# A hybrid decoder layer on one core: where the MLP operands of the first 1024 tokens are made, and how the last tiles are ordered and stored

## The chip, the cores and the metric

The kernel runs on one core of a Trainium2 chip. The metric is the device time of one execution in microseconds. Before the change the median of three runs is 1920.23 us (1919.95 to 1920.85). Lower is better.

The engines that matter: TensorE (PE in the profile, with its weight loads as PEld), VectorE (DVE), ScalarE (ACT), GpSimd (POOL), and the queues of SyncE (SP), ScalarE and GpSimd that issue transfers between HBM and the on-chip memory SBUF. PSUM is the memory that TensorE writes, here eight banks of 128 x 512 fp32.

## The reference

One decoder layer over 2048 tokens of width 1024, all in fp32:

```python
h = rms_norm(x, attn_norm_g)
z = h @ w_in                        # q, k, v and three convolution parts
q, k = rms_norm(q, q_norm_g), rms_norm(k, k_norm_g)
y_attn = swa_sink_attention(q, k, v, sinks)        # causal window of 128
y_conv = gate_b * short_conv(gate_c * xc, conv_w)  # three taps
y = concat([rms_norm(y_attn, attn_out_g), rms_norm(y_conv, conv_out_g)])
x = x + y @ w_out
hm = rms_norm(x, mlp_norm_g)
x = x + square(relu(hm @ w_up)) @ w_down
```

The norm ahead of the MLP needs, for each token, the root mean square over its 1024 values, and for each channel the gain `mlp_norm_g`. `w_up` is 1024 x 4096, `w_down` 4096 x 1024.

## The kernel before, in words

**Products in three parts.** An operand is kept as a high part, rounded to the format fp32r, and a low part, the rest. A product is three matmuls: high x high, high x low, low x high (`mm3`, L272). A matmul of 128 x 512 is the unit.

**Mixers.** The tokens go through norm, input projection, attention, convolution and output projection in four chunks of 512 (`NCHUNK`), each four tiles of 128 rows (`NT`). For each chunk `mixers` (L1022) walks the four attention blocks; between their steps it calls `fill`, which takes so many steps from the generator `besides` (L978): what is left of the chunk before (its attention half of the output projection, `rest`), then this chunk's convolution products (`conv_pair`), then the convolution half of the output projection interleaved with the preparation of the next chunk, then the next chunk's q, k, v products. How many steps each `fill` takes stands in the table `FILL`. Weights are reloaded for each chunk by `weights` (L239) on SP's queue.

**Order.** The kernel is written in one program order; a scheduler, working ahead of time on a model, sets each engine's order by priority. `ahead(i)` (L195) shifts the priority of the instructions in it by the entry `i` of `PRIO` for the current chunk; a positive number is earlier, a negative one later, counted in instructions. Each engine and each queue then works strictly in its order. A tile of SBUF or PSUM with a tag has as many places as `bufs` says; a new tile of the tag waits until a place is free. The row tiles `xt` (128 x 1024) have two places; the PSUM tag `tr` has one bank.

**Output projection** (`out_projection`, L899). For each half `dh` of the 512 output columns and each tile `t`, four steps of three matmuls fill a bank `pout`; VectorE then adds it, scaled by the row's norm, into the residual row `x1[t]` (L925). The convolution half (`half` 1) comes first, the attention half (`half` 0) after it. With the last column half of the attention half the row is complete: it is stored to `x1_dram` (L932), and for the first three chunks its row norm is computed into `rs_x1` (L935). The weights `w_wo` of the last tile of chunk 3 go into the two places of the tag `raw`.

**The MLP by seven products.** Both MLP products use the seven products of Strassen's method over halves of 512 tokens and 512 channels. For tokens 0 to 1023 (`tb` 0), let b11 and b21 be the two channel halves of the normed, transposed first 512 tokens and b12 and b22 those of the second 512. The seven operands are b11, b21, b22 and four differences. They are stored in HBM, in `xop_dram`, by `x_put` (L335) on SP, a block of 128 x 512 at a time, and loaded and split by `load_x` (L409) when a product needs them.

**Where these operands are made before** (`prepare_mlp`, L940). In chunk 3, beside the convolution half of the output projection. For each of the eight row tiles of chunks 0 and 1 it reloads the row from `x1_dram` (L952), scales it on VectorE by row norm and gain (L290), transposes it in two groups of four 128 x 128 blocks on TensorE (L316), copies each bank to SBUF on ScalarE (L317), and stores blocks (L341) or, for a tile of chunk 1, first makes the four differences on VectorE (`x_sums`, L355). The blocks stand in the places that the chunk's operand `h` has left. `rs_x1` and the row of gains `g_mlp` are read.

**Start of the MLP** (`begin_mlp`, L434): the first x operand and four blocks of `w_up` (`wu_first`, in the scratch tag `s2`) are loaded as the last steps of `besides`. Tokens 1024 to 2047 are prepared during the up products (`prepare_rest`, L1236), with the gain as a column `g_cols`.

**The end** (L1537 on). The down products go through 7 x 8 steps; each step has for each `tb` four banks of six matmuls (L1552). With the last step of the last product, `last` (L1496) adds each bank to the sum in SBUF on VectorE (L1498) and stores 128 x 512 on SP (L1494).

Of the kernel before, what the change touches and what calls it, by code (L numbers as in the profile page):

```python
# [16 lines left out]
P = 128  # L17
# [17 lines left out]
CH = 512  # L35
# [47 lines left out]


PRIO = (
# [5 lines left out]
)  # L91

FILL = (
# [9 lines left out]
def hymba_layer(  # L103
# [225 lines left out]
    def turned(xb, k, dst, g, rs_row):  # L329
# [2 lines left out]
        d3, r3 = dst.rearrange("p (t q) -> p t q", t=NT), rs_row.rearrange("p (q t) -> p t q", t=NT)  # L332
        nc.vector.scalar_tensor_tensor(d3, d3, g, r3, op0=ALU.mult, op1=ALU.mult)

    def x_put(tb, t, i, b):  # L335

        dst = xop_dram[tb][ORDER.index(i)]
        if tb:
            nc.sync.dma_start(dst[:, t * BW : (t + 1) * BW], b)
        else:  # L340
            nc.sync.dma_start(  # L341
                dst.rearrange("p (h t c) -> p h t c", h=2, t=NB)[:, :, t], b.rearrange("p (h c) -> p h c", h=2)
            )

    def rs_out(c):

# [1 line left out]
            rs_dram[c].rearrange("(p t) -> p t", p=P), rs_x1[:, c * NT : (c + 1) * NT]  # L348
        )

    def x_sums(tb, t, b11, b21, b12, b22, t1):


        def sub(i, dst, a, b):
            nc.vector.tensor_tensor(dst, a, b, op=ALU.subtract)  # L355
            x_put(tb, t, i, dst)

        x_put(tb, t, 3, b22)
        sub(5, t1, b12, b11)
        sub(6, b11, b22, t1)  # L360
        sub(7, b12, b22, b12)
        sub(4, b21, b21, b11)

    def gain_row(g, name):
        gb = row("gb", name, 1)
# [243 lines left out]
    with tc.tile_pool(name="mix_small", bufs=1) as mix_small, tc.tile_pool(name="mix", bufs=1) as mix:  # L609
# [289 lines left out]
        def out_projection(c, half, ys, rs, x1):  # L899

            for dh in range(2):
                cs = slice(dh * 512, (dh + 1) * 512)
                hl = ahead_parts.pop((half, dh), None) or out_weights(c, half, dh)
                if half and dh and c + 1 == NCHUNK:
                    ahead_parts[0, 0] = out_weights(c, 0, 0)
                w4 = [w.rearrange("p (i c) -> p i c", i=NCT) for w in hl]
                order = [(t, i) for t in range(NT) for i in range(NCT)]
                if half and not dh:

                    order = sorted(order, key=lambda x: (x[0] == NT - 1, x[1] == NCT - 1))  # L910
                pss = {}
                for t, i in order:
                    if not i:
                        pss[t] = bank("mm", f"pout{c}_{half}_{dh}_{t}")
                    ps = pss[t]

                    def y(s, i=i, t=t):
                        return ys[i][:, s, t * P : (t + 1) * P] if half else ys[t][:, s, i, :]

                    mm3(ps, y, lambda s, i=i: w4[s][:, i, :], i == 0, i == NCT - 1)  # L920
                    if i < NCT - 1:
                        yield
                        continue
                    with ahead(11):
                        nc.vector.scalar_tensor_tensor(  # L925
                            x1[t][:, cs], ps, rs[:, t : t + 1], x1[t][:, cs], op0=ALU.mult, op1=ALU.add
                        )
                        if dh and not half:
                            r = (c * NT + t) * P

                            eng = nc.gpsimd if c + 1 == NCHUNK else nc.sync
                            eng.dma_start(x1_dram[r : r + P, :], x1[t])  # L932

                            if c + 1 < NCHUNK:
                                norm_stats(x1[t], f"m{c}_{t}", rs_x1[:, c * NT + t : c * NT + t + 1])  # L935
                                if t + 1 == NT and c == NCHUNK - 2:
                                    rs_out(c)
                    yield

        def prepare_mlp(gb):  # L940


            xs = [pool.tile([P, 8, CH], F32, tag=f"h{i}", name=f"xm{i}", bufs=1) for i in range(2)]
            xts = {}

            halves = lambda w: w.rearrange("p (k c) -> p k c", k=2)

            def fetch(n):
                t, i = tiles[n]
                r = i * CH + t * P  # L950
                xt = xs[1][:, 3::4] if n % 3 == 2 else halves(row("xt", f"xt_m{i}_{t}", 2))
                nc.sync.dma_start(xt, halves(x1_dram[r : r + P, :]))  # L952
                with ahead(8):
                    scaled(xt, rs_x1[:, r // P : r // P + 1], halves(gb))
                xts[t, i] = xt

            tiles = [(t, i) for i in range(2) for t in range(NT)]
            for n in range(3):
                fetch(n)
            yield  # L960
            for n, (t, i) in enumerate(tiles):
                b = [xs[0][:, 2 * t + k] for k in range(2)]
                if i:
                    b += [xs[1][:, 4 * (t % 2) + k] for k in range(3)]
                with ahead(9):
                    for _ in raised(xts[t, i], lambda k: b[2 * i + k], f"m{i}_{t}"):
                        pass

                if n + 3 < len(tiles):
                    fetch(n + 3)  # L970
                if i:
                    x_sums(0, t, *b)
                else:
                    x_put(0, t, 1, b[0])
                    x_put(0, t, 2, b[1])
                yield

        def besides(c, before, h, yt, rc, x1, h_next, z_next):  # L978

            yield from before  # L980
            ssc = mix.tile([P, CH], F32, tag="ssc", name=f"ssc{c}", bufs=1)
            for j in range(2):
                yield from conv_pair(c, h, j, yt, ssc)
            for t in range(NT):
                r = (c * NT + t) * P
                xr = row("x1", f"x1_{c}_{t}", NT)
                nc.sync.dma_start(xr, xf[r : r + P, :])
                x1.append(xr)
            out = out_projection(c, 1, yt, rc, x1)
            if c + 1 < NCHUNK:  # L990
                h_next += parts(pool, "h", f"h{c + 1}")
                steps = prepare(xf, (c + 1) * CH, g_row[0], h_next, f"a{c + 1}")
            else:
                steps = prepare_mlp(gain_row(mlp_norm_g, "g_mlp"))
            for i, _ in enumerate(steps):
                yield
                for j in range(STEPS):
                    next(out, None)
                    yield
                    if (i, j) == PC:  # L1000
                        pc = bank("tr", f"pc{c}")
                        for t in range(NT):
                            nc.tensor.matmul(
                                pc[:, t : t + 1], ssc[:, t * P : (t + 1) * P], mean, start=True, stop=True
                            )
                        ms = mix_small.tile([P, NT], F32, tag="msc", name=f"ms_c{c}", bufs=1)

                        with tc.high_priority(offset=SOON):
                            if c:
                                nc.vector.tensor_copy(ms, pc[:, :NT])  # L1010
                                rsqrt(rc, ms)
                            else:
                                nc.vector.tensor_tensor(ms, pc[:, :NT], rs0_2, op=ALU.mult)
                                rsqrt(rc, ms)
                                nc.gpsimd.tensor_tensor(rc, rc, rs0, op=ALU.mult)
            yield from out
            if c + 1 < NCHUNK:
                yield from project_qkv(c + 1, h_next, z_next)
            else:
                begin_mlp()  # L1020
# [458 lines left out]
    def down_out(tb, p, ps, v):  # L1479
# [14 lines left out]
            eng.dma_start(of[r0 : r0 + P, (k - 1) * BW : k * BW], b[:, j])  # L1494

        def last(i, k, b):  # L1496
            for j in range(NB):
                nc.vector.tensor_tensor(b[:, j], ps[j], b[:, j], op=ALU.add)  # L1498
                put(i, k, b, j)

        def plus(a, b):

# [37 lines left out]
    for i, (p, g) in enumerate(steps):  # L1540
# [5 lines left out]
        for tb in range(NTB):  # L1546
            if first and p not in GOES_ON:
                ps[tb] = banks(tb, f"d{p}_{tb}")
            for j in range(NB):
                for k in range(2):  # L1550
                    for n, (a, b) in enumerate(((0, 0), (0, 1), (1, 0))):
                        nc.tensor.matmul(  # L1552
                            ps[tb][j],
                            fs[tb][:, a, k, j * P : (j + 1) * P],
                            w[:, b, k, :],
                            start=first and p not in GOES_ON and k + n == 0,
                            stop=last and k + n == 3,
                            skip_group_check=True,
                        )
            if i == NCG // 4:  # L1560
                down_out(tb, p, None, vs[tb])
            if last:
# [29 lines left out]
```

## Time and profile before

| | |
|---|---|
| median of three runs | 1920.23 us |
| lowest, highest | 1919.95, 1920.85 us |
| the profiled execution | 1921.78 us |
| its span, first to last instruction | 1920.1 us |
| mixers, up to the last pout product | to about 702.8 us |
| up products | 702.8 to 1306.6 us |
| down products | 1306.6 to 1916.1 us |
| HBM read, written | 286.87 MB, 125.83 MB |

How to read the rows that follow. A group has line, engine, operation, output <- inputs by the program's names, tile shape and count; then busy us and mean ns of one; then idle time of the engine just before, and what ended it. A row of waits has who waited for whom: us in total, how often, the longest. A row of a timeline has start, duration, engine, line, operation; SPq is SP's queue. A row of windows has for each engine busy us, the count in brackets, then the granted TensorE clock (1.00 is full), the share in which the 16 DMA engines were busy, and GB/s. A line number can be that of a helper that several places call.

### The profile page before, as it was taken

How to read it: one execution, taken by the hardware profiler on the slowest of the kernel's cores; microseconds unless marked ns; L12 is line 12 of the kernel's file. 1: busy time of each engine (PE TensorE's matmuls, PEld its weight loads, DVE VectorE, ACT ScalarE, POOL GpSimd, SP SyncE). 2: the span in 40 equal slices, each digit the busy share in tenths (PEclk: the TensorE clock that was granted, in tenths of full speed). 3: DMA queues.
4: the chain of work that ended last, by engine and by line, in shares of the span. 5: the costliest groups of instructions: out<-in, count | busy, mean ns of one | idle time of the engine just before them, and what ended most of it. 6: DMA issues, size and time to landing. Idle time of an engine off the chain costs nothing.

```text
span 1920.1 us, 24578 instructions
## 1 busy us (share of the span) xinstructions
PE 1910.4 (99%) x8927; PEld 1588.8 (83%) x8927; DVE 1205.4 (63%) x1849; ACT 829.3 (43%) x1564; POOL 275.6 (14%) x477
## 2 busy tenths in 40 slices
PE   9999999999999999999999999999999999999999
PEld 8888888888888778888888888888888888888887
DVE  4895656548556769999887766766534334457541
ACT  6565434335344446454555545554332332232320
POOL 2122212302221112233100111111000000100000
PEclk9999999999999999999999999999999999999999
DMA  8984944564563897778665444438954456766631
GB/s 305 340 313 115 333 185 175 209 230 161 201 263 135 285 345 255 219 226 254 214 223 202 163 161 146 150 138 318 367 203 146 139 169 226 284 224 214 210 132 55
DMA packets 233048, 414.32 MB, mean 216 GB/s; under 512 B 51672, under 2 KB 136160, under 8 KB 220128
## 3 DMA queue, kind: packets, MB, share of 16 engines
q1 hardware_dynamic: 204096, 336.98, 51.7%
q0 software_dynamic: 15424, 51.40, 6.9%
q10 hardware_dynamic: 13408, 24.39, 3.4%
q8 instruction: 70, 1.15, 0.2%
q14 instruction: 50, 0.41, 0.1%
HBM read 286.87 MB, written 125.83 MB: 215 GB/s over the span
## 4 chain that ended last, share of the span: by engine, by line
PE 65%; DMA 1%; DVE 0%; POOL 0%; ACT 0%; issue 0%; SPq 0%; POOLq 0%; ACTq 0%
PE d L1552 32%; PE u L1445 32%; PE pout L276 0%; PE pout L274 0%; PE pout L275 0%; DMA w_wo<-wo 0%; DMA xop<-xm 0%; PE pt_m L316 0%; DVE xm L355 0%; POOL pp_b L745 0%; PE po_b L784 0%; DVE xm L290 0%; DVE xt_m L290 0%; ACT xm L317 0%; DVE x L925 0%; DVE o_b L793 0%
## 5 line engine op out<-in xcount | busy, mean ns | idle before, releaser
L1445 PE MATMUL u<-op_x,wop 128*128 128x512 f32 x2688 | 610.2, 389 | 0.0
L1552 PE MATMUL d<-op_w,op_f 128*128 128x512 f32 x2688 | 609.6, 389 | 0.0
L1445 PEld LDWEIGHTS u<-op_x,wop 128*128 128x128 f32 x2688 | 504.4, 188 | 105.4 <-issue 0.7
L1552 PEld LDWEIGHTS d<-op_w,op_f 128*128 128x128 f32 x2688 | 504.4, 188 | 105.0 <-DVE op_f L406 0.3
L406 DVE TENSOR_TENSOR op_f<-op_f 128x1024 fp32r<-128x1024 f32 x112 | 136.9, 1224 | 235.7 <-ACT op_f L405 235.5
L405 ACT CAST op_f<-op_f 128x1024 fp32r<-128x1024 f32 x112 | 117.6, 1051 | 354.0 <-DMA op_f<-fop 353.1
L425 DVE TENSOR_TENSOR wop<-wu,wop 128x512 fp32r<-128x512 f32 x156 | 110.7, 711 | 36.3 <-ACT wop L424 18.5
L424 ACT CAST wop<-wu 128x512 fp32r<-128x512 f32 x156 | 95.9, 619 | 85.5 <-PE u L1445 81.5
L1181 POOL DMA_DIRECT2D fop<-s x96 | 51.9, 541 | 440.3 <-DVE s L1184 435.8
L1187 DVE TENSOR_TENSOR u<-u,u 128x512 f32<-128x512 f32 x128 | 87.8, 686 | 21.6 <-PE u L1445 21.5
L406 DVE TENSOR_TENSOR op_w<-raw,op_w 128x1024 fp32r<-128x1024 f32 x56 | 68.4, 1222 | 25.7 <-ACT op_w L405 25.4
L405 ACT CAST op_w<-raw 128x1024 fp32r<-128x1024 f32 x56 | 58.8, 1052 | 44.6 <-PE d L1552 21.6
L1193 ACT ACTIVATE u<-u 128x512 f32<-128x512 f32 x64 | 40.5, 633 | 64.5 <-DVE u L1187 62.5
L713 ACT ACTIVATE sc_b<-sc_b,ngm_b 128x128 f32<-128x128 f32 x128 | 49.6, 389 | 27.0 <-DVE ngm_b L710 27.0
L745 POOL TENSOR_SCALAR_AFFINE_SELECT pp_b<-pp_b 128x512 fp32r<-128x512 f32 x60 | 42.3, 717 | 130.7 <-ACT pp_b L738 72.1
L1394 POOL DMA_DIRECT2D wds<-raw x16 | 8.6, 534 | 328.3 <-DVE raw L1392 328.3
L424 ACT CAST wop<-wu_s 128x512 fp32r<-128x512 f32 x64 | 39.7, 621 | 32.0 <-PE u L1445 24.9
L274 PE MATMUL pout<-w_wo,yt_c 128*128 128x512 f32 x128 | 52.4, 410 | 0.0
L274 PE MATMUL pout<-w_wo,at_b 128*128 128x512 f32 x128 | 50.3, 395 | 1.7 <-DMA w_wo<-wo 1.5
L276 PE MATMUL pout<-w_wo,yt_c 128*128 128x512 f32 x128 | 51.8, 405 | 0.0
L425 DVE TENSOR_TENSOR wop<-wu_s,wop 128x512 fp32r<-128x512 f32 x64 | 44.9, 704 | 9.9 <-ACT wop L424 9.7
L275 PE MATMUL pout<-w_wo,yt_c 128*128 128x512 f32 x128 | 50.9, 398 | 0.0
(264 smaller groups left out, 3106.0 us busy)
## 6 DMA issues: line engine op xcount, KB each, us to landing
op_f<-fop SPq DMA_DIRECT2D x112, 512.0 KB, 4.3
raw<-in_w_down_dram SPq DMA_DIRECT2D x72, 512.0 KB, 4.2
wu<-in_w_up_dram SPq DMA_DIRECT2D x128, 256.0 KB, 4.2
w_wo<-wo SPq DMA_DIRECT2D x24, 1024.0 KB, 6.8
fop<-s POOLq DMA_DIRECT2D x96, 256.0 KB, 2.7
fop<-u ACTq DMA_DIRECT2D x64, 256.0 KB, 2.6
op_x<-xop SPq DMA_DIRECT2D x28, 512.0 KB, 7.0
w_q<-q SPq DMA_DIRECT2D x12, 1024.0 KB, 6.6
```

The lines of the kernel that those rows point to most:

```text
L274: nc.tensor.matmul(ps, st(0), mv(0), start=first, stop=False)
L275: nc.tensor.matmul(ps, st(0), mv(1), start=False, stop=False)
L276: nc.tensor.matmul(ps, st(1), mv(0), start=False, stop=last)
L405: nc.scalar.copy(op[:, 0], raw)
L406: nc.vector.tensor_tensor(op[:, 1], raw, op[:, 0].bitcast(F32), op=ALU.subtract)
L424: splits.append(nc.scalar.copy(hi, blk).ins)
L425: nc.vector.tensor_tensor(lo, blk, hi.bitcast(F32), op=ALU.subtract)
L713: nc.scalar.activation(sc[:, hd, :], sc[:, hd, :], AF.Exp, bias=ngm[:, hd : hd + 1], accum_out=den[:, hd : hd + 1])
L1181: eng.dma_start(fop_dram[tb][ORDER_DOWN.index(i)][n // 2][:, n % 2], b)
L1187: return nc.vector.tensor_tensor(dst, ps, b, op=ALU.add).ins
L1445: nc.tensor.matmul(pt, wops[i][:, a, k, :], xops[tb, p][k // 2][:, b, k % 2, :], start=p not in GOES_ON and k + j == 0, stop=k + j == NB + ...
L1552: nc.tensor.matmul(ps[tb][j], fs[tb][:, a, k, j * P : (j + 1) * P], w[:, b, k, :], start=first and p not in GOES_ON and k + n == 0, stop=l ...
```

## The change

- The operands of `tb` 0 are made by `x_first` as soon as a row of chunk 0 or 1 is complete and its norm is known, from the row in SBUF. As the program order goes, that is in the part of the output projection that runs under the next chunk, so in chunks 1 and 2.
- ScalarE scales the row by its norm into a row tile `xt`; TensorE transposes it in two groups; VectorE multiplies each bank by the gain column `g_cols` straight back into the row tile.
- A tile of chunk 0 stores its two blocks (b11, b21). A tile of chunk 1 takes a second row tile, reloads these two from `xop_dram`, stores b22, and makes the four differences in place, storing each.
- `ahead(12)` and `ahead(13)` put this work 150 instructions later in priority in every chunk. `FILL` stays.
- `prepare_mlp` and its row of gains go; in chunk 3 three empty steps are left beside the convolution half.
- In chunk 3 ScalarE instead of VectorE copies the sums of squares `ms` (L1010).
- The last projection tile of chunk 3 (first row tile of the second column half) takes its eight products with the high weight part first, then the four with the low part.
- In the very last bank of the down products, the last three matmuls of 512 columns become six of 256, by column halves; the last addition and store are made in two halves, the second stored on ScalarE's queue.

```diff
@@ PRIO: two more entries, -150 and -150, in each of the five rows
-    (40, 0, 160, -10, 30, 0, 10, -10, -20, 30, 0, 300),
+    (40, 0, 160, -10, 30, 0, 10, -10, -20, 30, 0, 300, -150, -150),
...
+    def x_piece(tb, t, i):
+        return xop_dram[tb][ORDER.index(i)].rearrange("p (h t c) -> p h t c", h=2, t=NB)[:, :, t]
...
-    def x_sums(tb, t, b11, b21, b12, b22, t1):
...
+    def x_first(c, t, x1):
+        xt = row("xt", f"xt_m{c}_{t}", 2)
+        r = c * NT + t
+        with ahead(12):
+            nc.scalar.activation(xt, x1, AF.Copy, scale=rs_x1[:, r : r + 1])
+            for k in range(2):
+                pt = bank("tr", f"pt_m{c}_{t}_{k}").rearrange("p (j q) -> p j q", j=NB)
+                b = xt[:, k * BW : (k + 1) * BW]
+                for j in range(NB):
+                    nc.tensor.transpose(pt[:, j], b[:, j * P : (j + 1) * P], ident)
+                nc.vector.tensor_tensor(
+                    b.rearrange("p (j q) -> p j q", j=NB),
+                    pt,
+                    g_cols[:, k * NB : (k + 1) * NB, None].to_broadcast([P, NB, P]),
+                    op=ALU.mult,
+                )
+        x11, x12 = (xt[:, k * BW : (k + 1) * BW] for k in range(2))
+        if not c:
+            x_put(0, t, 1, x11)
+            x_put(0, t, 2, x12)
+            return
+        before = row("xt", f"xb_{t}", 2)
+        b11, b21 = (before[:, k * BW : (k + 1) * BW] for k in range(2))
+        for i, b in ((1, b11), (2, b21)):
+            nc.sync.dma_start(b.rearrange("p (h c) -> p h c", h=2), x_piece(0, t, i))
+        b12, b22 = x11, x12
+        x_put(0, t, 3, b22)
+        with ahead(13):
+            for i, dst, a, b in ((5, b11, b12, b11), (7, b12, b22, b12), (6, b22, b22, b11), (4, b21, b21, b22)):
+                nc.vector.tensor_tensor(dst, a, b, op=ALU.subtract)
+                x_put(0, t, i, dst)
...
@@ out_projection
+                hi_first = dh and not half and c + 1 == NCHUNK
...
-                    mm3(ps, y, lambda s, i=i: w4[s][:, i, :], i == 0, i == NCT - 1)
+                    if hi_first and t == 0:
+                        sums = [(a, 0, k) for k in range(NCT) for a in range(2)] + [(0, 1, k) for k in range(NCT)]
+                        for n in range(3 * i, 3 * i + 3):
+                            a, s, k = sums[n]
+                            nc.tensor.matmul(
+                                ps, ys[t][:, a, k, :], w4[s][:, k, :], start=n == 0, stop=n + 1 == len(sums)
+                            )
+                    else:
+                        mm3(ps, y, lambda s, i=i: w4[s][:, i, :], i == 0, i == NCT - 1)
...
                                 norm_stats(x1[t], f"m{c}_{t}", rs_x1[:, c * NT + t : c * NT + t + 1])
+                                if c < 2:
+                                    x_first(c, t, x1[t])
...
-        def prepare_mlp(gb):
...
@@ besides
-                steps = prepare_mlp(gain_row(mlp_norm_g, "g_mlp"))
+                steps = range(PC[0] + 1)
...
-                                nc.vector.tensor_copy(ms, pc[:, :NT])
+                                if c + 1 == NCHUNK:
+                                    nc.scalar.copy(ms, pc[:, :NT])
+                                else:
+                                    nc.vector.tensor_copy(ms, pc[:, :NT])
...
@@ last
-            for j in range(NB):
+            ends = tb + 1 == NTB and p == ORDER_DOWN[-1]
+            for j in range(NB - ends):
                 nc.vector.tensor_tensor(b[:, j], ps[j], b[:, j], op=ALU.add)
                 put(i, k, b, j)
+            if ends:
+                r0 = (2 * tb + i - 1) * BW + j * P + P
+                for eng, c in ((nc.sync, slice(0, BW // 2)), (nc.scalar, slice(BW // 2, BW))):
+                    x = b[:, NB - 1, c]
+                    nc.vector.tensor_tensor(x, ps[NB - 1][:, c], x, op=ALU.add)
+                    eng.dma_start(of[r0 : r0 + P, (k - 1) * BW + c.start : (k - 1) * BW + c.stop], x)
...
@@ the down products
+                sums = [(k, n, slice(0, BW)) for k in range(2) for n in range(3)]
+                if i + 1 == len(steps) and tb + 1 == NTB and j + 1 == NB:
+                    sums[3:] = [(1, n, slice(h * BW // 2, (h + 1) * BW // 2)) for h in range(2) for n in range(3)]
+                for k, n, cs in sums:
+                    a, b = ((0, 0), (0, 1), (1, 0))[n]
...
```

More of the change, by code (lines that the diff above doesn't have):

```diff
@@ L340, in x_put @@
         else:
-            nc.sync.dma_start(
-                dst.rearrange("p (h t c) -> p h t c", h=2, t=NB)[:, :, t], b.rearrange("p (h c) -> p h c", h=2)
-            )
+            nc.sync.dma_start(x_piece(tb, t, i), b.rearrange("p (h c) -> p h c", h=2))
     def rs_out(c):
@@ L349, in rs_out @@
         )
-    def x_sums(tb, t, b11, b21, b12, b22, t1):
[L354 to L362, printed above, removed]
+    def x_first(c, t, x1):
[29 more added lines that the diff above has]
+                x_put(0, t, i, dst)
     def gain_row(g, name):
@@ L938, in out_projection @@
                     yield
-        def prepare_mlp(gb):
[L943 to L976, printed above, removed]
         def besides(c, before, h, yt, rc, x1, h_next, z_next):
@@ L1549, in hymba_layer @@
             for j in range(NB):
[L1550 to L1559, printed above, removed]
+                sums = [(k, n, slice(0, BW)) for k in range(2) for n in range(3)]
[3 more added lines that the diff above has]
+                    a, b = ((0, 0), (0, 1), (1, 0))[n]
+                    nc.tensor.matmul(
+                        ps[tb][j][:, cs],
+                        fs[tb][:, a, k, j * P : (j + 1) * P],
+                        w[:, b, k, cs],
+                        start=first and p not in GOES_ON and k + n == 0,
+                        stop=last and k + n == 3,
+                        skip_group_check=True,
+                    )
             if i == NCG // 4:
```

8 rows, old and new, of the table PRIO are left out of this document.

## The prediction

> **What bounds the kernel now.** I read the page's busy shares and matmul groups first, then the windows around the last mixer chunk, then who waited for whom on TensorE, then the chain that ended last.
>
> ```profile
> span 1920.1 us, 24578 instructions
> PE 1910.4 (99%) x8927; PEld 1588.8 (83%) x8927; DVE 1205.4 (63%) x1849; ACT 829.3 (43%) x1564; POOL 275.6 (14%) x477
> L1445 PE MATMUL u<-op_x,wop 128*128 128x512 f32 x2688 | 610.2, 389 | 0.0
> ```
>
> TensorE is busy almost always. Nothing in the change takes a matmul away, so only its idle time can be won. That idle time lies in one place:
>
> ```profile
> 640.00:660.00 20.00, 19.39 (x111) 15.28 (x110) 14.33 (x22) 9.84 (x20) 3.80 (x6) 1.00 0.98 322
> 660.00:680.00 20.00, 19.16 (x96) 15.33 (x94) 19.29 (x33) 7.95 (x12) 5.26 (x6) 1.00 0.91 290
> 680.00:700.00 20.00, 18.53 (x82) 15.02 (x82) 9.06 (x13) 8.49 (x12) 1.97 (x4) 1.00 1.02 343
> 450.00:550.00 100.00, 99.81 (x530) 84.44 (x529) 63.25 (x118) 42.40 (x104) 30.45 (x46) 1.00 0.51 199
> ```
>
> After the times, the first column is TensorE, the third VectorE; the last two are the DMA share and GB/s. The end of chunk 3 idles 0.61 + 0.84 + 1.47 = 2.9 us in 60, the 100 us of chunk 2's end only 0.2. In the first, VectorE is at 96% for 20 us and the DMA engines are full.
>
> ```profile
> PE pout L274 <- DMA w_wo<-wo: 1.5, 1, 1.5
> PE po_b L784 <- POOL pp_b L745: 0.5, 1, 0.5
> PE pt_m L316 <- DVE ms_c L1010: 0.4, 1, 0.4
> PE pt_m L316 <- ACT xm L317: 0.3, 1, 0.3
> PE pa_b L805 <- DVE o_b L800: 0.3, 1, 0.3
> PE pt_m L316 <- DVE xt_m L290: 0.2, 1, 0.2
> ```
>
> These six are 3.2 us. A matmul is shown for 0.389 us but in a full stream one starts every 597.94 / 2638 = 0.227 us (next fence), so each wait hides up to 0.16 us more: about 4.2 us in all.
>
> ```profile
> 680.55 8.54 DMA w_wo<-wo
> 689.13 0.96 PE pout L274 x3
> 702.80 597.94 PE u L1445 x2638
> ...
> 647.10 0.44 PE pt_m L316 x4
> ...
> 675.48 2.32 SPq L341 DMA_DIRECT2D xop<-xm  x3
> 677.89 2.60 SPq L419 DMA_DIRECT2D wu_first<-in_w_up_dram  x4
> 680.55 3.45 SPq L245 DMA_DIRECT2D w_wo<-wo  x2
> ```
>
> The first four are the chain (the fourth shows four transposes in 0.44 us), the others SP's queue. The last projection weights are issued at 680.55 because SP holds the xop stores before them, and those wait for VectorE. From 702.8 on TensorE streams without a gap.
>
> **The change, part by part.** Times are changes to the runs' median, 1920.23 us; the profiled execution had a span of 1920.1 us and took 1921.78 us, so 1.7 us lie around its span. No step alters those.
>
> *Last projection weights.* The operand step leaves chunk 3, so its 28 stores leave SP's queue ahead of w_wo, and 7.3 MB of stores and 4.2 MB of reloads leave the full DMA engines. The reordered tile also starts on the high half alone. What is late next is the four wu_first loads, still ahead of w_wo and waiting for scratch rows. The wait of 1.47 + 0.16 goes: **-1.6** (ends: 0 if those loads hold SP as long; -1.63).
>
> *Waits of the old transposes.* 0.4 + 0.3 + 0.2 + 3 x 0.16 = **-1.4** (ends 0 and -1.4). Copying ms on ScalarE takes one more VectorE step away.
>
> *Other waits there.* po_b and pa_b: 0.5 + 0.3 + 2 x 0.16 = 1.1.
>
> ```profile
> L355 DVE TENSOR_TENSOR xm<-xm 128x512 f32<-128x512 f32 x12 | 7.8, 688 | 0.0
> L290 DVE SCALAR_TENSOR_TENSOR xt_m<-xt_m,rs_x,g_mlp 128x1024 f32<-128x1024 f32 x6 | 7.6, 1280 | 2.6 <-DMA xt_m<-x_dram 2.5
> L283 ACT ACTIVATE junk_m<-x 128x1024 bf16<-128x1024 f32 x12 | 12.7, 1056 | 47.3 <-DVE x L925 43.5 <-POOL rs_x L191 3.2 <-DVE ngm_b L710 0.6
> L317 ACT COPY xm<-pt_m 128x512 f32<-128x512 f32 x16 | 9.4, 587 | 12.0 <-PE pt_m L316 8.6 <-DMA xop<-xm 3.3
> L307 DVE TENSOR_TENSOR h_h<-pt_a,h_h 128x512 fp32r<-128x512 f32 x24 | 16.5, 687 | 3.3 <-ACT h_h L306 3.0
> L302 PE MATMUL pt_a<-ident,xt_a 128*128 128x128 f32 x96 | 14.5, 274 | 0.5 <-DVE h_h L307 0.2 <-DVE ms_b L807 0.2
> ```
>
> VectorE loses 16 subtractions of 0.69 and 8 scalings of 1.28, 21 us, ScalarE 16 copies of 0.59, so the attention chain behind them runs earlier. But 64 transposes, 7 us of cover at 0.11 each, go as well. I take half: **-0.55** (ends: +1.1, the waits doubled without cover; -1.1).
>
> *The same work in chunks 1 and 2.* Eight tiles, each with a ScalarE scaling of 128x1024 (1.06 by L283, for two copies of 0.59), eight transposes, two VectorE products from PSUM of 0.69 (the form of L307), and for four of them four subtractions: 11 + 11 us of VectorE beside 63% (450 to 550). TensorE does as many transposes as before. Their waits: the nearest row is L302, whose 24 groups of four idled 0.5 us: 16 groups give 0.33, with hidden time **+0.4** (ends 0.3, and 1.4, the waits of pt_m again).
>
> *The stores and reloads.* These pass SP's queue: 8 stores in chunk 1, 20 stores and 8 reloads in chunk 2, behind which the next weights wait.
>
> ```profile
> 421.28 0.80 SPq L245 DMA_DIRECT2D w_wb<-wb  x2
> ...
> 447.41 0.39 PE L274 MATMUL pb_c<-h_h,w_wb 128*128 128x512 f32 x1
> ```
>
> I cost them at nothing: a weight pair issued at 421 is first used at 447, 26 us later, and no wait for a weight load but the one above is in TensorE's list. A store that waits in SP's queue for VectorE would have to hold it for most of these 26 us, less the landing, before TensorE saw it; from there each us counts in full. The row buffers have less cover: rival A.
>
> *The end.*
>
> ```profile
> 1916.12 0.69 DVE L1498 TENSOR_TENSOR d<-d,d 128x512 f32<-128x512 f32 x1 [0.67 <-PE d L1552]
> ...
> GB/s 183 429 196 0 126 410 271 0 44 403 353 6 0 372 410 25 0 315 410 82 0 233 410 164 0 145 410 252 0 69 416 322 0 0 0 0 0 0 0 0
> ...
> L799 DVE TENSOR_TENSOR o_b<-o_b 128x256 f32<-128x256 f32 x16 | 6.8, 425 | 2.6 <-ACT o_b L798 2.5
> ...
> 184.09 0.28 PE L276 MATMUL pz<-w_qkv,h_h 128*128 128x256 f32 x1
> 184.21 0.28 PE L274 MATMUL pz<-w_qkv,h_h 128*128 128x256 f32 x1
> ...
> fop<-u ACTq DMA_DIRECT2D x64, 256.0 KB, 2.6
> out_dram<-d SPq DMA_DIRECT2D x7, 256.0 KB, 2.0
> ```
>
> Six products of 256 columns at 0.12 replace three of 0.227: +0.04. The last addition is 0.42 in place of 0.69: -0.27. The last 256 KB moved at some 410 GB/s (the GB/s row has a slice every 0.325 us from 1908 to 1921), 0.64 us; half saves 0.32, the rest of the landing stays. **-0.55** (ends: +0.05 if ScalarE's queue, 2.6 against 2.0, is slower by 0.6; -0.6).
>
> The sum: -1.6 - 1.4 - 0.55 + 0.4 - 0.55 = -3.7: **1916.5 us**.
>
> **The rivals.**
>
> *A, slower: the two row buffers are late in chunk 2.* Each of its four tiles takes both buffers: one for the row, one for the reloaded half.
>
> ```profile
> 376.01 5.76 SPq L932 DMA_DIRECT2D x_dram<-x  x3
> ...
> DMA to landing us min/median/max: 3.3/4.6/8.7
> ...
> 460.64 0.60 PE L302 MATMUL pt_a<-ident,xt_a 128*128 128x128 f32 x4
> ...
> 345.00:430.00 85.00, 85.00 (x436) 72.19 (x435) 42.31 (x89) 30.66 (x89) 17.04 (x31) 1.00 0.66 248
> xop<-xm SPq DMA_DIRECT2D x28, 256.0 KB, 4.1
> ```
>
> A tile holds its rows for 4.7 us of engine work (1.06 + 2 x (0.44 + 0.69) + 2 x 0.69) and two landings L in a row, a store's and, once the rows are overwritten, another's. Four take 18.8 + 8L from the first finished tile at 376.0 (first line), and as an estimate 14 us more for its statistics and the lowered priority: 408.8 + 8L. Then chunk 3's rows come into the same buffers (4.6 us by the landings of xt_a, 2.3 more for the square and the scaling, 1.06 + 1.28) and are wanted by the transposes at 460.6, with the out projection's products queued behind these on TensorE. At L = 4.1, the median of the old stores, they are ready at 449; from L = 5.6 on TensorE waits 8 us for each further us. At L = 6.6 that is 8 us on the forecast: **1924.5 us**. For it: the stage gets 28 x 256 KB = 7.3 MB more in 85 us, a mean of 248 + 86 = 334 GB/s, and at 343 GB/s between 680 and 700 us the w_wo load took 8.54. Against: the old transposes had such stores before them on full engines, and of the waits above 0.3 us lie behind a copy that could have waited for one. The Trainium skill's page "DMA: Bandwidth & Descriptors", section "Specifications", gives a limit of about 358 GB/s for a core's HBM traffic; by that the stage would be 93% full and L long, so A would come true, while the GB/s row above has slices over 400, over that limit.
>
> *B: little is won in chunk 3.* SP stays held by wu_first, and less cover doubles po_b and pa_b: -1.4 + 1.1 + 0.4 - 0.55 = -0.45, **1919.8 us**. For it: the four wu_first loads take 2.6 us of SP right ahead of w_wo. Against: what held them in turn were the stores of 675.48.
>
> *C: all of it is won.* -1.63 - 1.4 - 1.1 - 0.6 = -4.7, with the new transposes wholly hidden: **1915.5 us**. For it: 21 us less on a VectorE at 96%.
>
> **How the numbers follow.** Forecast 0.46, A 0.25, B 0.10, C 0.19. About what a measurement of this kernel can tell from no change is 0.2%, 3.84 us: under 1916.4 is faster. The forecast's own range, 1915.8 to 1918, lies on both sides of that line; I give 0.23 to each, since the cover that goes is the term I know least and VectorE's relief speaks for the lower half: faster 0.23 + 0.19 = 0.42, same 0.23 + 0.10 = 0.33, slower 0.25. The range goes from 1914.8, below C by some error of the sum, to 1923.5, which takes in B and the milder cases of A, some 0.08 of its 0.25.
>
> **What would show it.** Right: no w_wo wait and no 2.9 us of idle in TensorE's last 60 us before the MLP; VectorE there well under 96%; the new transposes in chunks 1 and 2 with waits under half a us in all; a last addition of 0.4 us and an end about 0.5 us nearer to the last matmul. Wrong: TensorE waiting in chunk 2 or early chunk 3 for transposes of rows, or of xop landings (A); the w_wo wait still there behind wu_first (B); or a new idle stretch at the start of the MLP, which I costed at nothing since its operands are stored long before.

## The result and the profile after

The changed kernel takes 1929.24 us (median of 6 runs, 1927.54 to 1932.33) where the kernel before takes 1921.34 us (6 runs, 1919.95 to 1922.66, beside it): ratio 1.0044, interval 1.0031 to 1.0057. It is slower by some 0.4%; the forecast was 1916.5 us and the range ended at 1923.5. The profiled execution took 1928.08 us, with a span 6.2 us longer than before's; the medians lie 7.9 us apart.

The first lines of its page:

```profile
span 1926.3 us, 24572 instructions
PE 1912.2 (99%) x8930; PEld 1588.4 (82%) x8930; DVE 1203.8 (62%) x1857; ACT 828.1 (43%) x1557; POOL 271.8 (14%) x477
```

TensorE is busy 1.8 us longer than before (1910.4), and idle 4.4 us longer. Who waited for whom on TensorE (total us, times, longest):

```profile
PE pt_m L363 <- ACT xt_m L358: 2.7, 4, 1.0
PE pt_a L302 <- DVE ms_b L830: 2.0, 2, 1.8
...
PE pa_b L828 <- DVE o_b L823: 0.8, 2, 0.5
PE ptq_b L692 <- DVE sc_b L730: 0.8, 1, 0.8
PE pz L550 <- ACT w_q L588: 0.5, 1, 0.5
```

The 1.5 us for `w_wo` are gone; in their place TensorE waits for the new transposes (`pt_m` L363) and for chunk 3's first ones (`pt_a`). Where that lies is shown by the windows of before and then of after (chunk 1's out projection, chunk 2's, chunk 3's to the start of the MLP, and the part of the MLP's up products where a wait turns up; TensorE's busy time is the first column after the length):

```profile
200.00:300.00 100.00, 99.60 (x485) 82.10 (x484) 59.87 (x126) 44.44 (x130) 16.99 (x35) 1.00 0.66 256
380.00:500.00 120.00, 120.00 (x600) 100.22 (x599) 76.24 (x157) 55.03 (x163) 21.34 (x42) 1.00 0.57 214
600.00:710.00 110.00, 106.76 (x525) 87.01 (x524) 71.38 (x121) 45.02 (x104) 17.35 (x35) 1.00 0.78 266
900.00:950.00 50.00, 50.00 (x223) 41.39 (x222) 40.49 (x59) 24.97 (x44) 12.67 (x14) 1.00 0.65 219
```

```profile
200.00:300.00 100.00, 98.33 (x484) 80.12 (x483) 60.00 (x122) 43.20 (x120) 17.02 (x35) 1.00 0.76 277
380.00:500.00 120.00, 115.63 (x590) 94.88 (x589) 82.40 (x166) 57.61 (x159) 17.67 (x38) 1.00 0.76 269
600.00:710.00 110.00, 108.93 (x516) 89.94 (x515) 62.96 (x125) 43.36 (x110) 17.61 (x45) 1.00 0.51 180
900.00:950.00 50.00, 49.72 (x220) 40.80 (x219) 42.98 (x63) 24.38 (x42) 13.35 (x17) 1.00 0.71 238
```

Idle before: 0.40, 0.00, 3.24, 0.00 us. Idle after: 1.67, 4.37, 1.07, 0.28. Chunk 3 won 2.2 us; chunk 1 lost 1.3, chunk 2 4.4, the MLP 0.3: together +3.75 us. With the 0.5 us that `pz` waited in the first 20 us, in whose code nothing was edited, this is 4.2 of the 6.2 us. For the rest no row stands: ends of matmuls are modelled, so each wait shows up to 0.16 us short, and those below that don't show.

Chunk 2's loss in ScalarE's timeline (start, duration; in brackets how long ScalarE idled just before, and for what): the four scalings of chunk 1's rows.

```profile
384.14 1.15 ACT L358 ACTIVATE xt_m<-x,rs_x 128x1024 f32<-128x1024 f32 x1 [1.01 <-POOL rs_x L191]
415.47 1.15 ACT L358 ACTIVATE xt_m<-x,rs_x 128x1024 f32<-128x1024 f32 x1 [4.60 <-DVE sc_b L730]
432.18 1.15 ACT L358 ACTIVATE xt_m<-x,rs_x 128x1024 f32<-128x1024 f32 x1 [3.38 <-DMA xop<-xt_m]
446.72 1.15 ACT L358 ACTIVATE xt_m<-x,rs_x 128x1024 f32<-128x1024 f32 x1 [0.42 <-DMA xop<-xt_m]
```

And the stores of tile `xt_m` between 383 and 462 us (durations in ns, then the first and the last start):

```profile
L345 SPq DMA_DIRECT2D xop<-xt_m x12: 513/558/827, 404.8 to 456.4; - x12
...
DMA to landing us min/median/max: 2.4/4.2/6.7
```

Behind them, in the timelines, chunk 3's rows, and what TensorE's longest wait ended on:

```profile
460.12 0.81 SPq L401 DMA_DIRECT2D xt_a<-in_x_dram  x2
...
471.56 1.29 DVE L290 SCALAR_TENSOR_TENSOR xt_a<-xt_a,rs_a,g_attn 128x1024 f32<-128x1024 f32 x1 [0.17 <-POOL rs_a L191]
...
475.82 0.14 DVE L830 COPY ms_b<-pa_b 128x1 f32<-128x1 f32 x1
...
476.02 0.66 PE L302 MATMUL pt_a<-ident,xt_a 128*128 128x128 f32 x4 [1.79 <-DVE ms_b L830]
```

Each tile takes both row places until its stores have landed, so the next scaling comes some 15 us later (415, 432, 447). For the second the row names `sc_b`, which came last; the store of the first tile that held its place was issued at 411.59. TensorE's order is fixed: it reaches the transposes of the second to fourth tile before they are scaled.

The last store from `xt_m` is issued at 456.4, and chunk 3's rows are fetched at 460.12 and scaled until 472.9. The 1.8 us of waiting up to 476.0 did not end on these rows themselves: the transposes need the one bank of `tr`, and VectorE copies `pa_b` out of it (`ms_b`) only at 475.82, behind the late rows and other work in its queue. VectorE had idled 1.75 us up to 469.14 for the statistics of the first of them. That the lateness of the rows is what holds `ms_b` up is read from this order and not shown; that the wait goes when one of the two rows lies elsewhere is shown by e2.

The end, from the timeline of after:

```profile
1922.53 0.76 DVE L1505 TENSOR_TENSOR d<-d,d 128x256 f32<-128x256 f32 x2 [0.70 <-PE d L1562]
```

Both half additions run back to back (0.76 us for two) behind the last matmul; the first half is not early. The span ends 3.0 us after the last addition, 3.3 us before the change (1920.1 less 1916.81).

### The profile page after: what moved, and what is told of

It reads as the page before. It is cut to its first block, busy times and chain, and to the rows that moved or that the text cites. A ratio compares the mean times of both kernels' runs of the same rounds, so it can differ in the third digit from the quotient of the medians.

```text
span 1926.3 us, 24572 instructions
## 1 busy us (share of the span) xinstructions
PE 1912.2 (99%) x8930; PEld 1588.4 (82%) x8930; DVE 1203.8 (62%) x1857; ACT 828.1 (43%) x1557; POOL 271.8 (14%) x477
## 3 DMA queue, kind: packets, MB, share of 16 engines
q8 instruction: 70, 1.15, 0.2%
## 4 chain that ended last, share of the span: by engine, by line
PE 50%; DMA 1%; DVE 1%; issue 0%; ACT 0%; POOL 0%; SPq 0%; DVEq 0%; POOLq 0%
PE d L1562 31%; PE u L1445 19%; DMA raw<-in_w_down_dram 1%; DMA op_f<-fop 0%; POOL st_m L1119 0%; DVE raw L1392 0%; ACT op_w L428 0%; DVE u L1187 0%; DVE wop L448 0%; DVE op_f L429 0%; DVE s L1184 0%; ACT op_f L428 0%; DVE f L1184 0%; ACT wop L447 0%; ACT f L1190 0%
```

## The experiments

The theory after the result, called "places": the row buffers of chunk 1's tiles are held by stores and reloads, and this costs chunk 2 its 4 us. Rivals: the priority of the new step, VectorE or the stage being too full, SP's queue, and ScalarE's queue. Ratios are to the kernel before, run beside each.

**The small parts alone** (`e1_small_parts`): the kernel before with the reordered last projection tile and the halved last store, without `x_first`.

> The kernel before with only the two small parts: last projection tile high part first, last addition and store in halves. All theories: no new transposes, so no loss in chunks 1 and 2. The weights' wait of 1.6 us falls by 0.5 to 1.6 us, the end by 0.1 (the trace of the change shows both half additions after the last matmul): 0.6 to 1.7 us under before, ratio 0.9991 to 0.9997.

1921.18 us, ratio 0.9997 (0.9988 to 1.0006). The waits of TensorE:

```profile
PE pout L926 <- DMA w_wo<-wo: 1.1, 1, 1.1
```

The high part first takes 0.4 us off the wait for the weights (1.5 before); the change, which also takes the operand step out of chunk 3, has no such wait left. Neither small part costs or wins anything that can be measured.

**The reloaded row elsewhere** (`e2_reload_in_other_places`).

```diff
-        before = row("xt", f"xb_{t}", 2)
+        before = wop_pool.tile([P, D], F32, tag="wop", name=f"xb_{t}", bufs=NWOP)
```

> The changed kernel with the reloaded halves b11 and b21 in the four idle places of the tag wop, so that both xt places serve the rows of chunk 1. Theory places (each tile holds both places until its stores have landed, so the next tile's transposes wait in TensorE's order): the waits of the new transposes in chunk 2 fall from some 5 us with the hidden part to under 2, the time by 3 to 5 us. Rival load (the added VectorE work and transfers slow the stage): within 1 us of the change. Rival priority (150 later starts the chain too late): within 1.5 us of the change, since the first tile still starts late.

1925.55 us, ratio 1.0019 (1.001 to 1.0029). Its waits, then its window of chunk 2:

```profile
PE pt_m L363 <- ACT xt_m L358: 2.7, 2, 1.8
PE u L1445 <- DVE wop L448: 1.7, 1, 1.7
```

```profile
380.00:500.00 120.00, 117.40 (x600) 97.05 (x599) 85.03 (x171) 58.82 (x164) 19.86 (x40) 1.00 0.70 253
```

The `pt_a` wait of 1.8 us is gone and chunk 2 idles 2.60 instead of 4.37 us. The time fell as "places" had expected, but the 2.60 us are not under the 2 it had named: the scaled row still waits. The MLP stalls for 1.7 us.

**Priority 0 for the new step** (`e3_priority_0`): the two new columns of `PRIO` are 0 instead of -150.

> The changed kernel with 0 for the two -150 entries. Rival priority: the first tile's transposes come some 15 us earlier, the waits go, 4 to 6 us under the change. Theory places: the chain only starts earlier; its waits for stores stay at 2 to 4 us, but chunk 3's rows come 10 us earlier and the 2 us wait ahead of their transposes goes: 1 to 3 us under the change. Load: no change.

1928.8 us, ratio 1.0037 (1.0025 to 1.0049), no better than the change by more than the intervals allow, where "places" had expected 1 to 3 us less. The waits:

```profile
PE pt_m L363 <- ACT xt_m L358: 5.1, 4, 2.8
```

They move, they don't go: by the same windows chunk 1 idles 3.4 us instead of 1.7, chunk 2 1.7 instead of 4.4, with the `pt_a` wait gone. Starting 150 later isn't the cause; a priority of its own for each chunk was not tried.

**Without reloads and differences** (`e4_no_differences`): chunk 1's reload and its four subtractions are left out, the five stores kept with other contents.

> The changed kernel without the reload and the four subtractions for the tiles of chunk 1; all five stores stay, of undiffered blocks. Theory places: one landing per tile in place of two and two tiles in flight, so the waits of the new transposes in chunk 2 fall under 1 us and the time by 4 to 6 us. Load: 11 us of VectorE and 2 MB of transfers less, which are 5% of what the stage has: under 1.5 us less. Priority: 1 to 2 us less.

1923.17 us, ratio 1.0006 (0.9997 to 1.0015). Its window of chunk 2:

```profile
380.00:500.00 120.00, 119.20 (x609) 98.60 (x608) 77.24 (x158) 58.90 (x164) 20.15 (x40) 1.00 0.69 252
```

Chunk 2 idles 0.80 us, 3.6 less than with the change, as "places" had expected. The cost hangs on the reload and the differences; whether by the places or by VectorE's load, e9 tells.

**Scaling on GpSimd** (`e5_scale_on_gpsimd`).

```diff
-            nc.scalar.activation(xt, x1, AF.Copy, scale=rs_x1[:, r : r + 1])
+            nc.gpsimd.tensor_scalar(xt, x1, rs_x1[:, r : r + 1], None, op0=ALU.mult)
```

> The row scalings of x_first go from ScalarE to GpSimd; row places and everything else as in the change. Theory 'queue': in the change each scaling stands in ScalarE's queue ahead of the copies that the attention needs and waits there for rs_x; with it gone, the wait of ptq_b for sc_b (0.8 us at 211 us) is gone and the time falls by 0.8 to 2 us against the change (1927 to 1928.5). Theory 'places': what is lost in chunk 2 comes from the two row buffers; the waits of pt_m and pt_a there (about 4.3 us shown in the change) stay within 1.5 us. Rival 'slow engine': GpSimd takes longer for a row than ScalarE's 1.15 us, so transposes come later and the waits of pt_m grow by over 1.5 us; the time is that of the change or above.

1938.54 us, ratio 1.0092 (1.0079 to 1.0105). The scalings (shortest, median, longest in ns), then the waits, in an execution that took 1942.31 us:

```profile
L358 POOL TENSOR_SCALAR xt_m<-x,rs_x x8: 2845/2864/3303, 209.8 to 452.3; 128x1024 f32<-128x1024 f32 x8
```

```profile
PE pt_m L363 <- POOL xt_m L358: 11.0, 5, 3.2
PE u L1445 <- DVE wop L448: 4.3, 1, 4.3
```

The rival "slow engine" holds: 2.86 us a row instead of 1.15, and `pt_m` waits 11.0 us. The theory "queue" was right on the wait and wrong on the time: `ptq_b` no longer waits, which shows that the scaling in ScalarE's queue made it. How it did so stands in the timelines of ScalarE, VectorE and TensorE of the change:

```profile
209.37 1.15 ACT L358 ACTIVATE xt_m<-x,rs_x 128x1024 f32<-128x1024 f32 x1 [1.01 <-POOL rs_x L191]
210.43 0.62 ACT L727 COPY sc_b<-psc_b 128x256 f32<-128x256 f32 x2
...
210.81 0.90 DVE L730 COPY_PREDICATED sc_b<-later,psc_b 128x128 f32<-128x128 int32 x4 [2.01 <-ACT sc_b L727]
...
211.46 0.63 PE L692 MATMUL ptq_b<-ident,z 128*128 128x128 f32 x4 [0.77 <-DVE sc_b L730]
```

ScalarE idles 1.01 us at the head of its queue for GpSimd's `rs_x`, scales for 1.15, and only then copies the scores that VectorE and, behind it, TensorE want.

**Own places for both rows, GpSimd** (`e6_own_places`): as e5, with `xt_m` and `xb` both in `wop` places.

> Both rows that chunk 1's operand step needs (the scaled row and the reloaded one) lie in other places (four instead of two for the four tiles' rows of a stage), and the scaling is on GpSimd. Theory 'places' with 'queue': no wait of pt_m or pt_a over 0.4 us is left in chunk 2, none of ptq_b in chunk 1; what remains is the gain of chunk 3 (about 2.8 us), so 1919 to 1922, that is 0 to -2.5 against before. Rival 'stage': chunk 2 itself is too full (VectorE and 7 MB more of traffic), so waits of the same size turn up at other tiles and the time stays at 1925 or above.

1927.71 us, ratio 1.0029 (1.0017 to 1.0041); one of its 7 runs took 2739.42 us, why is open, and without it the median is 1927.18. The waits:

```profile
PE pt_m L363 <- POOL xt_m L358: 5.8, 2, 4.2
```

The places take 11 us off e5 (1938.54 to 1927.71), but two waits for GpSimd's scalings are left, and the expected 1919 to 1922 failed. The time lies where the rival "stage" had put it; e9 tells the two apart.

**Half of the move** (`e7_half_moved`): only chunk 0's rows are made early (`if c < 1:`); chunk 1's are made in chunk 3 by the old step, with chunk 0's halves reloaded there.

> Chunk 0's rows are made early as in the change; chunk 1's rows are made in chunk 3 as before, with the rows of chunk 0 reloaded there for the differences. Theory 'places': nothing in chunk 2 needs the row buffers for stores and reloads, so chunk 2 (400 to 500 us) is as in before (idle under 1 us); chunk 1 keeps its cost (1 to 2 us) and chunk 3 wins part of its 2.9 us: 1919.5 to 1922.5. Rival 'cover': chunk 3's remaining step waits as before and chunk 1's cost comes on top: 1922.5 to 1925.

1923.84 us, ratio 1.0014 (1.0005 to 1.0022). Its windows:

```profile
200.00:300.00 100.00, 98.17 (x482) 79.97 (x481) 59.84 (x121) 43.00 (x119) 17.02 (x35) 1.00 0.77 275
380.00:500.00 120.00, 120.00 (x600) 100.21 (x599) 76.02 (x154) 54.86 (x161) 20.23 (x41) 1.00 0.58 217
600.00:710.00 110.00, 107.89 (x516) 88.09 (x515) 72.80 (x131) 44.01 (x106) 21.29 (x43) 1.00 0.74 259
```

Chunk 2 idles 0.00 us, chunk 1 1.83 and chunk 3 2.11: chunk 2's loss belongs to chunk 1's rows, chunk 1's to chunk 0's. The time lay in the rival's range, since chunk 3 keeps waits of its old step.

**Stores alone** (`e8_stores_alone`): the rows are stored as they are; scalings, 64 transposes, products, reloads and differences are left out.

> Chunks 0 and 1 store their rows as they are into the MLP's operands (the same 28 stores at the same places); the scalings, transposes, gain products, reloads and differences are left out, and with them 64 transposes (about 7 us of TensorE at 0.11 us each). Theory: queue and traffic of the stores cost nothing, so chunks 1 and 2 have no wait of more than 0.4 us, and the time is before less 7 (transposes) and less 2.8 (chunk 3): 1910 to 1913. Rival 'queue SP': the stores in SP's queue hold weight loads up; then waits for weights appear in chunks 1 and 2 and the time is above 1914.

1914.05 us, ratio 0.996 (0.9949 to 0.9972). Windows of chunks 1 and 2:

```profile
200.00:300.00 100.00, 99.59 (x480) 82.01 (x478) 60.23 (x124) 42.48 (x126) 17.23 (x35) 1.00 0.73 279
380.00:500.00 120.00, 120.00 (x599) 100.18 (x598) 73.89 (x153) 54.61 (x162) 20.71 (x41) 1.00 0.64 247
```

No new idle time: 28 stores at these places cost nothing. The time is 1 us above what was expected and so touches the rival's 1914, but the rival's waits for weights are not there; a 0.9 us wait in the MLP makes up most of it.

**Own places for both rows, ScalarE** (`e9_own_places_scalar`).

```diff
-        xt = row("xt", f"xt_m{c}_{t}", 2)
+        xt = wop_pool.tile([P, D], F32, tag="wop", name=f"xt_m{c}_{t}", bufs=NWOP)
...
-        before = row("xt", f"xb_{t}", 2)
+        before = wop_pool.tile([P, D], F32, tag="wop", name=f"xb_{t}", bufs=NWOP)
```

> Chunk 1's scaled rows and reloaded rows both lie in other places (as in e6), the scaling is on ScalarE as in the change. Theory 'places': the 5.8 us that pt_m still waited for xt_m in e6 were GpSimd's 2.87 us a row and its queue, so here pt_m waits for at most 0.5 us in chunk 2; the waits of ptq_b (0.8 us each) at 211 and 390 us come back, and the time is 1923 to 1925, like e4 which has no reloads at all (1923.17). Rival 'order': TensorE's order holds the transposes ahead of conv products whatever the places, so pt_m still waits for 2 us or more in chunk 2 and the time is that of e2 (1925.5) or above.

1922.92 us, ratio 1.0007 (0.9998 to 1.0016). All its waits of TensorE in chunk 2, and two windows:

```profile
PE ptq_b L692 <- ACT sc_b L727: 0.8, 1, 0.8
```

```profile
380.00:500.00 120.00, 119.22 (x609) 98.77 (x608) 87.21 (x173) 58.76 (x164) 21.45 (x41) 1.00 0.74 263
...
900.00:950.00 50.00, 48.04 (x212) 39.44 (x211) 40.01 (x58) 23.98 (x42) 11.82 (x14) 1.00 0.66 220
```

With every reload and difference in place, VectorE busy for 87.21 us instead of the change's 82.40, `pt_m` and `pt_a` wait for nothing. The places are the cause of chunk 2's loss, not VectorE, the traffic or TensorE's order by itself. What is left is the queue's 0.8 us, once in each of chunks 1 and 2, and 1.96 us in the MLP. This execution took 1925.47 us, 2.6 us more than the median, so the wait in the MLP need not be in the others.

**As e9, and a tile later** (`e10_own_places_tile_later`).

```diff
-                                if c < 2:
-                                    x_first(c, t, x1[t])
+                                if c < 2:
+                                    for s in range(max(t - 1, 0), t + t // (NT - 1)):
+                                        x_first(c, s, x1[s])
```

> As e9, and x_first of a tile is called one tile later (the last two together), so that the row statistics are ready long before the scaling is issued. Theory 'head of queue': the scaling no longer holds ScalarE's queue while it waits for rs_x, so ptq_b does not wait in chunks 1 and 2, nor pt_m; what is left is chunk 3's gain less a stall at the start of the MLP's products: 1919 to 1922. Rival: what is issued later collides with chunk 2's own preparation (the last two tiles together) or with chunk 3's, and new waits of 1 us or more stand there: 1923 or above.

1922.1 us, ratio 1.0002 (0.9993 to 1.0011): the time of before. Its windows:

```profile
200.00:300.00 100.00, 99.31 (x490) 81.35 (x489) 61.24 (x123) 43.12 (x120) 17.43 (x35) 1.00 0.74 267
380.00:500.00 120.00, 120.00 (x614) 100.04 (x613) 86.83 (x175) 58.49 (x164) 20.55 (x40) 1.00 0.72 263
600.00:710.00 110.00, 109.03 (x512) 90.25 (x513) 64.09 (x124) 42.99 (x105) 17.42 (x43) 1.00 0.53 190
900.00:950.00 50.00, 49.43 (x218) 40.59 (x217) 39.80 (x58) 24.02 (x42) 11.22 (x14) 1.00 0.63 210
```

Idle 0.69, 0.00, 0.97, 0.57, in all 2.23 us against before's 3.64. These windows win some 1.4 us, but the time doesn't show it (before took 1920.98 us beside it); the interval can't tell so little. The scalings hardly moved, each first one still waits 1.01 us for `rs_x`, and from e9 the time differs by less than the intervals; this doesn't settle the queue.

**The change a tile later** (`e11_tile_later`): the edit of e10 without that of e9.

> The change with x_first of a tile called one tile later and nothing else; two row places as in the change. Theory 'places': the last two tiles of chunk 1 come together and need four rows from two places, and chunk 3's rows come behind them: waits of pt_m or pt_a of 4 us or more stay in chunk 2, time 1926 to 1931. Rival 'order only': if it was only the early place of scaling and transposes in the queues, the waits go and the time is 1919 to 1923.

1932.33 us, ratio 1.0055 (1.0042 to 1.0069). The waits:

```profile
PE pt_m L363 <- ACT xt_m L358: 4.9, 3, 2.4
```

Order without places doesn't help: the rival "order only" falls.

**As e7, a tile later** (`e12_half_moved_tile_later`).

> As e7 (chunk 0 early, chunk 1's rows in chunk 3), with x_first one tile later. Theory 'head of queue': the 1.0 us at 211 us (ptq_b) and most of the 1.4 us at 250 us (pt_m) of e7 go, 1921 to 1923 (e7 1923.84). Rival: no change within 1 us, the waits only move.

1926.46 us, ratio 1.0027 (1.0016 to 1.0037), above e7, though the intervals overlap, and outside both expectations. Its scalings of chunk 0's last two tiles, from ScalarE's timeline:

```profile
248.89 1.15 ACT L358 ACTIVATE xt_m<-x,rs_x 128x1024 f32<-128x1024 f32 x1 [11.71 <-DMA xop<-xt_m]
255.70 1.15 ACT L358 ACTIVATE xt_m<-x,rs_x 128x1024 f32<-128x1024 f32 x1 [4.27 <-DMA xop<-xt_m]
```

The third and fourth tile wait for the stores of the first two already in chunk 1, where there is no reload, and TensorE waits 2.2 us for one of these scalings.

## Why the prediction was wrong, step by step

- **Last projection weights, -1.6; old transposes, -1.4.** Neither wait is in after's list. By e1 only 0.4 us of the first is due to the order of the products, so most of it is due to the move. For the second this is not shown: e1 leaves the old step in chunk 3, and its list has 0.2 us of `pt_m` waits where before's has 0.9, so they can shrink without the move.
- **Other waits there, -0.55.** About nothing: `po_b` lost its 0.5 us, `pa_b` went from 0.3 to 0.8. The doubling without cover that I had as an end came for one of the two. The three terms, -3.55 in all, gave 2.2 us of idle time in chunk 3 and some tenths that don't show.
- **The same work in chunks 1 and 2, +0.4 (at most 1.4).** This is the step that failed: 1.3 + 4.4 us of idle time. I sized it by L302, whose rows are never stored: their places come free with their transposes, and VectorE scales them. So that row holds the cost of a transpose, but not that of a place held until a landing, nor of a scaling in ScalarE's queue. The new rows show both: a scaling at the head of ScalarE's queue waits for statistics just made (0.8 us of TensorE's time, gone in e5), and a row place is free only when its stores have landed (gone in e9, whose time is 6 to 7 us under the change's by median and ratio).
- **Rival A, 0.25.** Its mechanism came true, its price not. Its 4.7 + 2L a tile is 13.1 us at the measured L = 4.2, against some 15 seen. But it let TensorE lose time only at chunk 3's rows, and there 1.8 us were lost, behind VectorE's queue; chunk 2's own transposes wait earlier, since they stand in TensorE's order ahead of products that were ready. The argument against A was unsound: the old step's stores read `xs`, places of their own, and so never held a row buffer, while the new stores read the row buffers themselves. The code says so (the `b` of `prepare_mlp`, the `xt` of `x_first`).
- **Stores and reloads in SP's queue, nothing.** Right: e8 has no new idle time with the stores, and e10 none in chunk 2 with the reloads as well.
- **The end, -0.55.** About -0.2: from the start of the last bank's addition to the end of the span 4.0 us before (1920.1 less 1916.12) and 3.8 after (1926.3 less 1922.53). I let the first half be added ahead of the last products; it waits for all of them.
- **The start of the MLP, nothing.** Off by 0.3 us here, and by 0.6 to 4.3 us in most of the variants, some 220 us into the up products. TensorE waits there for a weight that VectorE splits, and VectorE's queue stands ahead of it for a late load of `raw`, a piece of `w_down`: 3.02 us before, without a wait of TensorE, 4.67 in the change, 5.76 in e9, 7.47 in e5. Why this load is late was not tried.

Of the versions, e10 keeps what the change takes from chunk 3 and pays nearly nothing elsewhere, and its time is that of before. None beats the kernel before by what can be measured.

## What to carry to other kernels

When a step moves, ask of each buffer that it writes what reads it last: an operation in place that is then stored ties the buffer to a landing (4.2 us here), while a copy into another place had set it free. A step that is costed by "the same work elsewhere" needs a row of work whose buffers come free in the same way, since a late input is paid at every engine whose order is fixed. And an instruction that waits for a value just computed holds up the ready work behind it in its queue (1.01 us on ScalarE here, 0.77 on TensorE); whether it pays to put it behind that work, no run here has shown.

## What the hardware did that was not expected

A wait costs more than its length once TensorE's clock falls. The windows of e11 behind its two longest waits, 2.43 us up to 254.16 and 1.89 us up to 434.70 (the clock is the last column but two):

```profile
254.00:256.00 2.00, 1.84 (x8) 1.66 (x9) 0.62 (x1) 0.11 (x1) 0.00 (x0) 0.50 0.46 132
256.00:258.00 2.00, 2.00 (x10) 1.61 (x10) 1.04 (x3) 0.59 (x1) 1.09 (x2) 0.65 0.78 301
...
434.00:436.00 2.00, 1.30 (x6) 1.20 (x7) 0.21 (x1) 1.16 (x2) 0.00 (x0) 0.72 0.74 283
436.00:438.00 2.00, 2.00 (x9) 1.60 (x7) 1.08 (x2) 0.63 (x1) 0.00 (x0) 0.50 0.96 373
438.00:440.00 2.00, 2.00 (x10) 1.68 (x9) 1.29 (x2) 0.00 (x0) 0.00 (x0) 0.93 0.55 197
```

Inside such a stretch finer windows show 0.50 and outside it 1.00, so a window of 2 us at 0.72 is 1.12 us at 0.50. The granted clock is thus 0.50 for 2.0 + 1.4 and for 1.12 + 2.0 + 0.28 us: 3.4 us each time. By finer windows it was at 0.50 for 3.4 us after e12's wait of 2.2 us too, and 6.8, twice that, after e6's of 4.2 and e5's of 4.33. At half the clock 3.4 us hold work for 1.7 us: e11's profiled execution took 2.5 us more than the change's (1930.6 against 1928.08) with about the same idle time in the four windows (7.55 against 7.39).

In e9 a wait of 1.96 us left the clock at 1.00, and so did the change's 1.8 us, so length alone doesn't decide. The Trainium skill's page "TensorE: Matmul & The Clock Gate", section "What's actually happening", has the clock fall to half after an idle window of about 3.4 us that runs freely. That the stretches last 3.4 us or twice that, and that length alone doesn't decide, agrees with a free-running window; that 1.89 us of idle time can be enough doesn't agree with a window that is idle throughout.
